# A diffusion layer on one core: split head sums, gated weight columns, a second store queue, and an order for pooled differences

## The chip, the core and the metric

The kernel runs on one core of a Trainium2 chip, as one launch. The metric is the time of one execution on the device in microseconds (us). A core has engines that run side by side and wait for one another through semaphores. In the profile PE is the matrix engine (TensorE), PEld its weight loads, DVE the vector engine, ACT the scalar engine, POOL the GpSimd engine and SP the engine that here issues nearly all DMAs. "SPq" marks what an engine's queue issues or waits for, a DMA for example.

## The reference

One trunk layer over 256 latent tokens and 256 context tokens of width 2048, all in float32. The parts that matter here, with the reference's own names:

```
h   = modulate(x, ...);  p = h @ w_in            # q, k, v, pool input, gate logits
heads = diff_attention(q, k_all, v_all, lam)     # 8 heads, value width 128
heads = rmsnorm(heads, subln_w) * (1 - lam_init) # mean of squares over the 128 values of a head
y_a = heads @ w_a_up
y_b = multiscale_pool(p[pool], ...) @ w_b_up     # 4 groups, windows 2, 4, 8, 16
x   = x + ga * ((g_a * y_a + g_b * y_b) @ w_o)
x   = x + gm * (square(relu(modulate(x, ...) @ w_ff1)) @ w_ff2)
```

`multiscale_pool` takes, for each token and each window, the mean of the input over the window (fewer tokens at both ends of the sequence) minus the input itself, and multiplies the difference by a 256 x 256 matrix of its group. `ga` and `gm` are vectors of 2048 gates that a product with `w_mod` makes.

## The kernel before

**Numbers in two halves.** PE multiplies operands of type fp32r faster than plain float32 ones. So most float32 operands are split: `hi` is the value cast to fp32r (ACT, line 245 for weights) and `lo` the rest (DVE, line 246). A product is three: hi·hi, lo·hi and hi·lo (`mm3`, lines 275 to 278, and `xstat`, lines 454, 455 and 460).

**Weights as a stream.** All weights come in chunks of 128 x 1024 floats (512 KB) in an order written out by hand (`plan`, lines 133 to 173). `load_next` (line 199) takes the next one: SP starts the DMA into one of 6 `raw` buffers, ACT casts it into one of 3 `whi` buffers, DVE subtracts into one of 3 `wlo` buffers. A chunk is loaded two chunks ahead of its use. Beside the stream a generator (`late_gen`, line 597) loads 128 chunks of `w_mod` for the gates; DVE accumulates them (`late_part`, lines 628 and 630), and POOL folds the rows with DMAs. `wchunk` calls `tick` once for each chunk, and work given to `later(n, ...)` comes up n chunks later.

**Stages.** First the modulation of both token sets with part of q and k (to about 190 us), then the other projections, attention and pooling side by side with the gates' products (to about 660 us), the output product `w_o`, and eight blocks of the MLP, each `ff1` (16 chunks) and then `ff2` (16 chunks: four groups `g` of 512 columns, four chunks each). Attention is a generator that `run` (line 871) advances between the matmuls of the other parts.

**Order.** A planner puts the instructions of each engine in order at build time: of those that it believes ready it takes the one that stands first in the program. Instructions passed through `pin` keep their program order among the pinned ones of the same engine. On the chip each engine then runs its list strictly in that order, and an instruction that waits holds up all behind it on its engine.

**The places that the change touches.**

- Head sums: `av` (line 715) makes two heads into one PSUM bank `ob`. ACT copies it (`osb`, 725) and squares it (`osq`, 727), POOL clamps the squares (728). Five chunks later `norm` multiplies them by `mean`, a 128 x 128 tile filled with 1/128, in one float32 product (732); ACT and DVE make a reciprocal root of it (`rsq`) and scale the heads.
- Pooled differences: `pooling` (764) makes a group's input in one bank, ACT copies it into two `za` tiles (787), POOL adds shifted copies of it (792). Four chunks later (eight for the last window) `pool_diff` (797) corrects the first tokens (803, pinned), the last ones (805, not pinned, windows 4 to 16) and subtracts the input (807, not pinned).
- Last block: POOL first multiplies the sums `acc` by `gm` and adds `x1` (1079, 1080). For each group of columns, `ff2` multiplies the bank by `gm` (1067), adds `acc` (1068) and stores (1069, SP's queue). The last group, g = 3, does so in two halves of 256 columns for each of the two token tiles, and its last two chunks are taken together (`last=2`), so that the first token tile is ready before the second.
- `work` tiles (line 75) are 9 buffers of 128 x 512 floats that attention, pooling and the head sums share.

Of the kernel before, what the change touches and what calls it, by code (L numbers as in the profile page):

```python
# [11 lines left out]
F32 = mybir.dt.float32  # L12
F32R = mybir.dt.float32r
AF = mybir.ActivationFunctionType
ALU = mybir.AluOpType
AX = mybir.AxisListType

P = 128
D = 2048
KT = D // P  # L20
T = 256
# [3 lines left out]
SQ_MAX = 3.39e38  # L25
# [23 lines left out]
def layer(ctx: ExitStack, tc, a, out):  # L49
    nc = tc.nc  # L50
    pool = ctx.enter_context(tc.tile_pool(name="sb", bufs=1))
    psum = ctx.enter_context(tc.tile_pool(name="ps", bufs=8, space=bass.MemoryType.PSUM))
    rows = ctx.enter_context(tc.tile_pool(name="rows", bufs=3, space=bass.MemoryType.DRAM))
    pe, gp = nc.tensor, nc.gpsimd
    pin = tc.keep_in_program_order
# [14 lines left out]
    act, vec, pe, sp = Engine(nc.scalar, ordered), Engine(nc.vector, ordered), Engine(nc.tensor, ordered_pe), nc.sync  # L70

    def bank(name):
        return psum.tile([P, 512], F32, tag="ps", name=name)

    def work(name, shape=None, dt=F32):
        return pool.tile(shape or [P, 512], dt, tag="w2", name=name, bufs=9)

    def s16(name, shape, dt=F32):
        return pool.tile(shape, dt, tag="s16", name=name, bufs=7)

    def s8(name, shape, dt=F32):
        return pool.tile(shape, dt, tag="s8", name=name, bufs=2)
# [7 lines left out]
    mods = {}  # L90
# [6 lines left out]
    def later(n, fn):  # L97

        waiting.append([n, fn])
# [15 lines left out]
    def raw_chunk(src, n=1024):  # L115
        raw = pool.tile([P, n], F32, tag="raw", name="raw", bufs=6)
        sp.dma_start(raw, src)
        return raw
# [61 lines left out]
    def x1_tile():  # L180
        if not x1s:
            x1s.append(s16("x1", [P, 2, D]))
        return x1s[0]
# [5 lines left out]
    def mod_raw(f, i):  # L189

        home = f % 2 if f > 7 else f % 4
        if home == 0:
            return pool.tile([P, 1024], F32, tag="raw", name="raw", bufs=6)
        n = 2 if home == 1 else 4
        if i % n == 0:
            wide[0] = (s8 if home == 1 else s16)("raw", [P, n, 1024])
        return wide[0][:, i % n, :]

    def load_next():
        key, rate = stream[len(loaded)]  # L200
        src = a[key[0]]
        for i in key[1:] if key[0] != "prq" else ():
            src = src[i]
        if key[0] == "prq":
            for dst, names in prq[key[1]]:
                nc.gpsimd.dma_start(dst, a["prq"][:, PRQ[names[0]][0]:PRQ[names[-1]][1]])
            loaded.append((key, None, None))
            return
        if key[0] in ("cT", "x"):
            dst = cT[:, 4 * key[1]:4 * key[1] + 4, :] if key[0] == "cT" else x1_tile()[:, key[1], key[2] * 512:key[2] * 512 + 512]  # L210
            nc.sync.dma_start(dst, src)
            loaded.append((key, None, None))
            return
        n = src.shape[-1]
        if key[0] == "w_m":
            raw = mod_raw(*key[1:])
            sp.dma_start(raw, src)
            loaded.append((key, raw, raw))
            return
        if key[0] in ("w_k", "w_q") and key[1] == 0:  # L220
            raw = pool.tile([P, n], F32, tag="aT", name="raw", bufs=2)
            sp.dma_start(raw, src)
            loaded.append((key, raw, raw))
            return
        raw = raw_chunk(src, n)
        if key == ("w_ff1a", 0):
            hi, lo = (pool.tile([P, n], F32R, tag="aT", name=nm, bufs=2) for nm in ("hi0", "lo0"))
        elif key == ("w_o", 3, 4):
            pair = s8("pair", [P, 2, 1024], F32R)
            hi, lo = pair[:, 0, :], pair[:, 1, :]  # L230
        elif key in (("w_ff1a", 2), ("w_ff1a", 3)):
            i = 2 * (key[1] - 2)
            if i == 0:
                early.append(s16("early", [P, 4, 1024], F32R))
            hi, lo = early[0][:, i, :], early[0][:, i + 1, :]
        elif key == ("w_ff1a", 1):
            halves = [[work(nm, dt=F32R) for nm in ("hi1", "lo1")] for _ in range(2)]
            for h in range(2):
                split(*halves[h], raw[:, h * 512:h * 512 + 512])
            loaded.append((key, *zip(*halves)))  # L240
            return
        else:
            hi = pool.tile([P, n], F32R, tag="whi", name="whi", bufs=3)
            lo = pool.tile([P, n], F32R, tag="wlo", name="wlo", bufs=3)
        act.copy(hi, raw)  # L245
        vec.tensor_sub(lo, raw, hi.bitcast(F32))  # L246
        loaded.append((key, hi, lo))
        credit[0] += rate if late[0] is not None else 0.0
        credit_rate[0] = rate
        while credit[0] >= 1.0:  # L250
            credit[0] -= 1.0
            if "gm" not in mods or mods["gm"] is not None or key[0] in ("w_ff1a", "w_ff1"):
                next(late[0], None)
# [17 lines left out]
    def split(hi, lo, src):  # L271
        act.copy(hi, src)  # L272
        vec.tensor_sub(lo, src, hi.bitcast(F32))  # L273
# [19 lines left out]
    prm = pool.tile([P, PRM_W], F32, tag="prm", name="prm")  # L293
# [12 lines left out]
    vec.memset(ebias, -32.0 * math.log(2.0))  # L306
    epsb = pool.tile([P, 1], F32, tag="epsb", name="epsb")
    vec.memset(epsb, EPS * 2.0 ** -64)
    mean = pool.tile([P, P], F32, tag="mean", name="mean")
    vec.memset(mean, 1.0 / P)  # L310


# [241 lines left out]
    for f in range(KT):  # L554
        if f % 2 == 0:
            ps = bank("mod")
# [158 lines left out]
    def av(h):  # L715
        assert h < values[0]
        if h % 2 == 0:
            ob[h // 2] = bank("ob")
        ps = ob[h // 2]
        for kc in range(4):  # L720
            pe.matmul(ps[:, (h % 2) * T:(h % 2) * T + T], v[:, kc, h * P:h * P + P], aTs[h][:, kc, :],
                      start=(kc == 0), stop=(kc == 3))
        if h % 2 == 1:
            osb = work("osb")
            act.copy(osb, ps)
            sq = work("osq")
            act.activation(sq, ps, AF.Square)
            gp.tensor_scalar(sq, sq, SQ_MAX, None, ALU.min)

            def norm():  # L730
                sp = bank("osum")
                pin(pe.matmul(sp, mean, sq, start=True, stop=True))
                r = rsq(sp, 512, 1.0)

                vec.scalar_tensor_tensor(r, sp, SUM_MAX / P, r, ALU.is_lt, ALU.mult)
                vec.scalar_tensor_tensor(osb, osb, sub8, r, ALU.mult, ALU.mult)
                o2 = osb.rearrange("p (a t) -> p a t", t=T)
                split(oT[:, 0, h - 1:h + 1, :], oT[:, 1, h - 1:h + 1, :], o2)
                heads[0] += 2

            later(5, norm)
# [55 lines left out]
    def pool_diff(g, w, ps, sums):  # L797

        d = work("d")
        n0, n1 = w // 2, w // 2 - 1  # L800
        e0 = PRM["edge"][0] + sum(x - 1 for x in WINDOWS[:g]) * 2
        for i, s in enumerate(sums):
            pin(vec.tensor_mul(s[:, 0:n0], s[:, 0:n0], prm[:, e0:e0 + n0]))
            if n1:
                vec.tensor_mul(s[:, T - n1:T], s[:, T - n1:T], prm[:, e0 + n0:e0 + n0 + n1])
            sl = slice(i * T, i * T + T)
            vec.scalar_tensor_tensor(d[:, sl], s, 1.0 / w, ps[:, sl], ALU.mult, ALU.subtract)
        diff.append((work("dh", dt=F32R), work("dl", dt=F32R)))
        later(1, partial(split, *diff[-1], d))

# [100 lines left out]
    for g in range(4):  # L911
        bs = [bank(f"wo{t}") for t in range(2)]
# [38 lines left out]
    acc = s16("acc", [P, 2, D])  # L951
# [98 lines left out]
    def ff2(b):  # L1050
        at = [acts[b]]
        for g in range(4):
            bs = [bank(f"f2_{t}") for t in range(2)]
            for _ in xstat(("w_ff2", b, g), bs, [(at, 0), (at, 1)], nk=4, last=2 if b == 7 and g == 3 else 1):
                pass
            gs = slice(g * 512, g * 512 + 512)
            for t in range(2):
                if b == 0:
                    act.copy(acc[:, t, gs], bs[t])
                elif b < 7:  # L1060
                    vec.tensor_add(acc[:, t, gs], bs[t], acc[:, t, gs])  # L1061
                else:
                    n = 256 if g == 3 else 512
                    for c in range(0, 512, n):
                        o = work("o", [P, n])
                        cs = slice(g * 512 + c, g * 512 + c + n)
                        vec.tensor_mul(o, bs[t][:, c:c + n], mods["gm"][:, cs])
                        vec.tensor_add(o, o, acc[:, t, cs])
                        nc.sync.dma_start(out[t * P:t * P + P, cs], o)

    ff1_first(bs)
    for b in range(8):
# [114 lines left out]
```

## Time and profile before

| | |
|---|---|
| median of 3 runs | 1454.63 us (1454.03 to 1455.06) |
| the profiled execution, its own time | 1452.88 us |
| its span, first to last instruction | 1451.0 us |
| PE busy | 1431.2 us (99%), 7448 matmuls |
| PEld busy | 1178.8 us (81%) |
| DVE busy | 975.3 us (67%) |
| ACT busy | 674.6 us (46%) |
| POOL busy | 173.4 us (12%) |
| DMA | 355.22 MB, mean 245 GB/s |

A row of a timeline has the start in us from the beginning of the span, the duration in us, the engine, the line, the operation, what it writes and reads, its shape and how many are merged in the row; in brackets stands for how long the engine was idle just before, and what ended that. A row of busy times by stretch has the stretch, its length, the busy us and the count of each engine, then the granted clock of PE, the busy share of the DMA engines and GB/s. Matmuls are pipelined, so a matmul's duration is longer than its distance from the next one. Both PE operand types are shown as f32 where they are inputs.

### The profile page before, as it was taken

To read this page: it belongs to the slowest core of one execution; us is meant where nothing else is said; L and a number is where in the kernel's file an instruction comes from. 1 tells how busy PE (TensorE), PEld (TensorE's weight loads), DVE (VectorE), ACT (ScalarE), POOL (GpSimd) and SP (SyncE) were. 2 spreads that over 40 slices of the span, in tenths; PEclk is the share of its full clock that TensorE was granted. 3 is DMA by queue.
4 is the path that set the end of the run, shared out by engine and by line. 5 is a ranking of instruction groups with operands and counts; after the bars stand their busy time and mean duration, and the time that the engine had idled before them with its cause. 6 is when DMAs were issued, how large, how long until landed. Compare 5 with 4: busy or idle time off the path is not lost.

```text
span 1451.0 us, 19755 instructions
## 1 busy us (share of the span) xinstructions
PE 1431.2 (99%) x7448; PEld 1178.8 (81%) x7448; DVE 975.3 (67%) x1218; ACT 674.6 (46%) x901; POOL 173.4 (12%) x192
## 2 busy tenths in 40 slices
PE   6999999999999999999999999999999999999998
PEld 4667887788888888888878888888888888888887
DVE  4567785668788778887766665656657555555675
ACT  5235345466644444444545545445354453544432
POOL 1001110101421111110101100011000110000260
PEclk9999999999999999999999999999999999999999
DMA  9996683345599999999746676777767765565563
GB/s 379 409 407 255 207 312 120 96 132 162 178 302 333 351 312 348 345 359 328 228 153 216 232 244 227 252 236 249 253 228 241 217 204 189 190 202 187 191 196 123
DMA packets 100975, 355.22 MB, mean 245 GB/s; under 512 B 12864, under 2 KB 13520, under 8 KB 100880
## 3 DMA queue, kind: packets, MB, share of 16 engines
q1 hardware_dynamic: 96624, 345.19, 68.8%
q0 software_dynamic: 4256, 8.77, 2.7%
q8 instruction: 58, 0.95, 0.3%
q14 instruction: 37, 0.30, 0.1%
HBM read 347.61 MB, written 2.17 MB: 241 GB/s over the span
## 4 chain that ended last, share of the span: by engine, by line
PE 91%; DMA 7%; DVE 1%; ACT 0%; issue 0%; SPq 0%; POOL 0%; DVEq 0%
PE f L1037 14%; PE f L455 8%; PE f L454 8%; PE f L460 8%; PE f L1039 7%; DMA raw<-in_w_m_dram 6%; PE pg L454 4%; PE pg L455 4%; PE pg L460 4%; PE pyy L454 2%; PE pyy L455 2%; PE pyy L460 2%; PE v L455 2%; PE v L454 2%; PE v L460 2%; PE wo L454 2%
## 5 line engine op out<-in xcount | busy, mean ns | idle before, releaser
L246 DVE TENSOR_TENSOR wlo<-raw,whi 128x1024 fp32r<-128x1024 f32 (+1 forms) x430 | 527.8, 1238 | 295.8 <-ACT whi L245 194.9
L245 ACT CAST whi<-raw 128x1024 fp32r<-128x1024 f32 (+1 forms) x430 | 450.4, 1048 | 519.3 <-PE f L455 183.8
L1037 PE MATMUL f<-h,whi 128*128 128x512 f32 x896 | 213.9, 391 | 0.0
L455 PE MATMUL f<-whi,act 128*128 128x512 f32 x512 | 199.3, 389 | 0.0
L454 PE MATMUL f<-whi,act 128*128 128x512 f32 x512 | 199.2, 389 | 0.0
L1037 PEld LDWEIGHTS f<-h,whi 128*128 128x128 f32 x896 | 165.0, 188 | 32.2
L460 PE MATMUL f<-wlo,act 128*128 128x512 f32 x512 | 136.8, 389 | 0.0
L1039 PEld LDWEIGHTS f<-h,wlo 128*128 128x128 f32 x896 | 114.9, 191 | 4.4
L1039 PE MATMUL f<-h,wlo 128*128 128x256 f32 x896 | 116.2, 283 | 0.0
L460 PEld LDWEIGHTS f<-wlo,act 128*128 128x128 f32 x512 | 96.1, 188 | 20.0
L455 PEld LDWEIGHTS f<-whi,act 128*128 128x128 f32 x512 | 96.2, 188 | 19.8
L454 PEld LDWEIGHTS f<-whi,act 128*128 128x128 f32 x512 | 96.1, 188 | 19.7
L454 PE MATMUL pg<-whi,hL 128*128 128x512 f32 x256 | 100.8, 394 | 0.0
L455 PE MATMUL pg<-whi,hL 128*128 128x512 f32 x256 | 99.7, 389 | 0.0
L1047 POOL TENSOR_TENSOR rsq<-relu 128x512 f32<-128x512 f32 x28 | 29.1, 1040 | 455.4 <-ACT relu L1046 445.2
L630 DVE SCALAR_TENSOR_TENSOR sb<-raw,sil,sb 128x1024 f32<-128x1024 f32 x60 | 76.7, 1278 | 0.0
L460 PE MATMUL pg<-wlo,hL 128*128 128x512 f32 x256 | 68.4, 389 | 0.0
L454 PEld LDWEIGHTS pg<-whi,hL 128*128 128x128 f32 x256 | 48.1, 188 | 10.5 <-ACT whi L245 0.4
L455 PEld LDWEIGHTS pg<-whi,hL 128*128 128x128 f32 x256 | 48.1, 188 | 10.1 <-issue 0.2
L460 PEld LDWEIGHTS pg<-wlo,hL 128*128 128x128 f32 x256 | 48.1, 188 | 10.0
L273 DVE TENSOR_TENSOR act<-rsq,act 128x512 fp32r<-128x512 f32 x28 | 19.3, 689 | 53.0 <-ACT act L272 53.0
L1061 DVE TENSOR_TENSOR acc<-f,acc 128x512 f32<-128x512 f32 x48 | 30.9, 686 | 20.4 <-PE f L460 20.4
(283 smaller groups left out, 2180.1 us busy)
## 6 DMA issues: line engine op xcount, KB each, us to landing
raw<-in_w_ff_dram SPq DMA_DIRECT2D x240, 512.0 KB, 4.3
raw<-in_w_m_dram SPq DMA_DIRECT2D x64, 512.0 KB, 10.2
raw<-in_w_ga_dram SPq DMA_DIRECT2D x32, 512.0 KB, 4.4
raw<-in_w_gb_in_dram SPq DMA_DIRECT2D x32, 512.0 KB, 5.3
raw<-in_w_cm_dram SPq DMA_DIRECT2D x32, 512.0 KB, 5.8
raw<-in_w_ga_in_dram SPq DMA_DIRECT2D x32, 512.0 KB, 5.6
raw<-in_w_sm_dram SPq DMA_DIRECT2D x32, 512.0 KB, 5.6
raw<-in_w_o_dram SPq DMA_DIRECT2D x32, 512.0 KB, 5.3
```

The lines of the kernel that those rows point to most:

```text
L245: act.copy(hi, raw)
L246: vec.tensor_sub(lo, raw, hi.bitcast(F32))
L273: vec.tensor_sub(lo, src, hi.bitcast(F32))
L454: pe.matmul(banks[t], tok(h, k, 0, tt), wt, start=k == 0, stop=False)
L455: pe.matmul(banks[t], tok(h, k, 1, tt), wt, start=False, stop=False)
L460: pe.matmul(banks[t], tok(h, k, 0, tt), wt, start=False, stop=k == 2 * nk - 1)
L630: pin(vec.scalar_tensor_tensor(o, raw, sil[:, 0, k:k + 1], o, ALU.mult, ALU.add))
L1037: pe.matmul(ps, hi[:, kk * P:kk * P + P], both(h2, k), start=k == 0, stop=False)
L1039: pe.matmul(ps[:, T:2 * T], los[k // 8][:, k % 8 * P:k % 8 * P + P], act_slice(h2, k, 0), start=False, stop=k == KT - 1)
L1047: gp.tensor_mul(sq, r, r)
L1061: vec.tensor_add(acc[:, t, gs], bs[t], acc[:, t, gs])
```

## The change

Four edits:

1. **Head sums.** POOL's clamp goes. DVE makes two fp32r tiles from the squares, `sh` (clamped) and `sl` (the rest of the clamped square), and `norm` multiplies both by the mean tile, now of type fp32r, into the same bank: two products for one float32 product.
2. **Gated weights.** When one of the last four chunks (`w_ff2`, block 7, g = 3) has landed, DVE multiplies it in place by the 512 gates `gm` of its columns, ahead of the cast. The last group's bank then needs only the addition of `acc`.
3. **Store.** The second half of each of the last group's two stores is issued on ACT's queue, the rest stays on SP's.
4. **Pooled differences.** Lines 805 and 807 are pinned like line 803.

```
+        if key[:3] == ("w_ff2", 7, 3):
+            r3 = raw.rearrange("p (k f) -> p k f", k=2)
+            vec.tensor_mul(r3, r3, mods["gm"][:, 1536:2048].unsqueeze(1).broadcast_to([P, 2, 512]))
...
-    mean = pool.tile([P, P], F32, tag="mean", name="mean")
+    mean_r = pool.tile([P, P], F32R, tag="mean", name="mean")
+    mean = mean_r.bitcast(F32)
...
-            gp.tensor_scalar(sq, sq, SQ_MAX, None, ALU.min)
+            sh, sl = (work(nm, dt=F32R) for nm in ("osh", "osl"))
+            vec.tensor_scalar(sh, sq, SQ_MAX, None, ALU.min)
+            vec.scalar_tensor_tensor(sl, sq, SQ_MAX, sh.bitcast(F32), ALU.min, ALU.subtract)
...
-                pin(pe.matmul(sp, mean, sq, start=True, stop=True))
+                pin(pe.matmul(sp, mean_r, sh, start=True, stop=False))
+                pin(pe.matmul(sp, mean_r, sl, start=False, stop=True))
...
-                vec.tensor_mul(s[:, T - n1:T], s[:, T - n1:T], prm[:, e0 + n0:e0 + n0 + n1])
+                pin(vec.tensor_mul(s[:, T - n1:T], s[:, T - n1:T], prm[:, e0 + n0:e0 + n0 + n1]))
...
-            vec.scalar_tensor_tensor(d[:, sl], s, 1.0 / w, ps[:, sl], ALU.mult, ALU.subtract)
+            pin(vec.scalar_tensor_tensor(d[:, sl], s, 1.0 / w, ps[:, sl], ALU.mult, ALU.subtract))
...
-                        vec.tensor_mul(o, bs[t][:, c:c + n], mods["gm"][:, cs])
-                        vec.tensor_add(o, o, acc[:, t, cs])
-                        nc.sync.dma_start(out[t * P:t * P + P, cs], o)
+                        if g < 3:
+                            vec.tensor_mul(o, bs[t][:, c:c + n], mods["gm"][:, cs])
+                            vec.tensor_add(o, o, acc[:, t, cs])
+                        else:
+                            vec.tensor_add(o, bs[t][:, c:c + n], acc[:, t, cs])
+                        (nc.scalar if c > 0 else nc.sync).dma_start(out[t * P:t * P + P, cs], o)
```

## The prediction

> **What bounds the kernel now.** I read the page's busy times and its chain of waits first, then the busy times by stretch, and then the timelines of the places that the change touches.
>
> ```profile
> PE 1431.2 (99%) x7448; PEld 1178.8 (81%) x7448; DVE 975.3 (67%) x1218; ACT 674.6 (46%) x901; POOL 173.4 (12%) x192
> ...
> PE 91%; DMA 7%; DVE 1%; ACT 0%; issue 0%; SPq 0%; POOL 0%; DVEq 0%
> ```
>
> ```profile
> 0.00:50.00 50.00, 37.62 (x285) 24.79 (x286) 25.00 (x56) 22.75 (x37) 5.89 (x15) 0.93 0.99 387
> ...
> 200.00:300.00 100.00, 99.46 (x453) 74.76 (x452) 66.74 (x121) 49.06 (x94) 8.21 (x5) 1.00 0.43 137
> 300.00:400.00 100.00, 99.27 (x641) 86.01 (x640) 76.96 (x115) 64.10 (x112) 24.84 (x41) 1.00 0.52 162
> 400.00:500.00 100.00, 100.00 (x452) 83.12 (x451) 79.57 (x77) 45.32 (x52) 17.55 (x22) 1.00 0.96 327
> ...
> 1400.00:1451.00 51.00, 46.34 (x205) 38.04 (x203) 31.19 (x37) 15.06 (x15) 8.14 (x5) 0.98 0.44 145
> ```
>
> PE carries the chain. It is idle for 12.4 us in the first 50 (50 minus 37.62), which the change doesn't touch, for some 1.3 us between 200 and 400 us, and for 4.7 us at the end. So only three things can make this kernel faster: less work on PE, the stalls between 200 and 400 us, and the tail. And anything that makes PE wait costs its full length. The span of 1451.0 us with 1.9 us around it is the profiled time, 1452.88; the median of the runs, 1454.63, is 1.75 above it. I make the sum against the profile and take the difference off the median.
>
> **Head sums, on PE.** The fourth of the four products, and its neighbours:
>
> ```profile
> 396.40 0.39 PE L455 MATMUL pg<-whi,hL 128*128 128x512 f32 x1
> 396.63 1.07 PE L460 MATMUL pg<-wlo,hL 128*128 128x512 f32 x4
> 397.54 1.02 PE L732 MATMUL osum<-osq,mean 128*128 128x512 f32 x2
> 397.99 0.79 PE L454 MATMUL pg<-whi,hL 128*128 128x512 f32 x1
> ```
>
> The product before ends at 397.70 (396.63 plus 1.07), the float32 product at 398.56 (397.54 plus 1.02): 0.86 us. An fp32r product of the same shape costs 0.23, the distance of the first two rows' starts. Two of them are 0.46, so 0.40 is saved each time, 1.6 us in four. Bounds: nothing, if fp32r against the mean tile ran no faster, to 2.5 us, if the second product hid wholly (4 times 0.63); all fp32r rows of this shape go at 0.23, so I take 1.6. The products stay pinned on PE, so they now wait for DVE where they waited for POOL.
>
> **Head sums, on DVE and POOL.** Nearest rows for the two new DVE steps are a one-source step of twice the width and a two-source step of the same width; what POOL loses stands below:
>
> ```profile
> L628 DVE TENSOR_SCALAR gm_bc<-raw,sil x2: 748/748/748, 766.5 to 955.8; 128x1024 f32<-128x1024 f32 x2
> L288 DVE SCALAR_TENSOR_TENSOR rq_t<-osum,rq_t x4: 684/690/691, 314.8 to 401.3; 128x512 f32<-128x512 f32 x4
> L728 POOL TENSOR_SCALAR osq<-osq x4: 1491/1559/2480, 282.6 to 388.6; 128x512 f32<-128x512 f32 x4
> ```
>
> `sh` is half of 748, some 0.4, and `sl` 0.69: 1.1 us for each pair of heads, 4.4 us on DVE, for 6 to 7 us less on POOL. The shortest time from squares to product is the third pair's:
>
> ```profile
> 363.46 1.57 POOL L728 TENSOR_SCALAR osq<-osq 128x512 f32<-128x512 f32 x1 [14.52 <-ACT osq L727]
> ...
> 368.23 1.02 PE L732 MATMUL osum<-osq,mean 128*128 128x512 f32 x2
> ```
>
> The squares exist by 363.4 and the product starts at 368.23. 1.1 us fits into 4.8, so I cost it at nothing. If the cover is gone, the pinned product waits and PE with it, at most 1.1 us a pair. The two tiles take one `work` buffer more through those five chunks; that is a risk below.
>
> **Pooled differences.** This is the one place in the attention stage where PE waits for long:
>
> ```profile
> DVE za L805 <- POOL za L792: 5.9, 3, 3.0
> ...
> PE pin L278 <- DVE wlo L246: 0.7, 1, 0.7
> ```
>
> ```profile
> 364.61 0.68 DVE L246 TENSOR_TENSOR wlo<-raw,whi 128x512 fp32r<-128x512 f32 x1
> 368.25 0.75 DVE L805 TENSOR_TENSOR za<-za,prm 128x3 f32<-128x3 f32 x2 [2.96 <-POOL za L792]
> 368.94 1.23 DVE L246 TENSOR_TENSOR wlo<-raw,whi 128x1024 fp32r<-128x1024 f32 x1
> ...
> 369.21 0.28 PE L277 MATMUL pin<-hL,whi 128*128 128x256 f32 x1
> 370.22 0.39 PE L278 MATMUL pin<-hL,wlo 128*128 128x256 f32 x1 [0.73 <-DVE wlo L246]
> 370.44 0.28 PE L276 MATMUL pin<-hL,whi 128*128 128x256 f32 x1
> ```
>
> The planner put line 805, which is not pinned, far ahead of its group's line 803. It holds DVE for 2.96 us until POOL's sums are done; the subtraction of the next weight chunk, behind it, comes at 368.94, though DVE was through with all else at 365.3 (364.61 plus 0.68), and PE stops. The two PE products ought to follow at 0.12 (369.33 and 369.45); the second comes at 370.44: 1.0 us lost. Pinned behind 803, line 805 comes where its sums have long been there. DVE gets back 5.9 us, which more than pays for the 4.4 above, and PE 1.0. Line 807 depended on 803 already, so its pin moves little; behind it wait `late_part` steps with their raw buffers, and each group's steps are 0.7 us longer in one piece (two small multiplications move there). What is late next is the same subtraction, 1.1 us later than it could be because the third pair's `sh` and `sl` come just ahead of it: at about 366.4 it is done by 367.6, 1.7 us before PE needs it at 369.33. Bounds: nothing, if another wait stands there, to 1.3 us, all the idle of that stage; I take 1.0.
>
> **Gated weights.** What counts is whether four multiplications of about 1.22 us (the price of line 246, same shape) find room ahead of their casts.
>
> ```profile
> 1429.15 1.05 ACT L245 CAST whi<-raw 128x1024 fp32r<-128x1024 f32 x1 [1.66 <-PE f L455]
> ...
> 1437.31 1.06 ACT L245 CAST whi<-raw 128x1024 fp32r<-128x1024 f32 x1 [1.66 <-PE f L455]
> ```
>
> ```profile
> 1430.24 1.22 DVE L246 TENSOR_TENSOR wlo<-raw,whi 128x1024 fp32r<-128x1024 f32 x1 [1.31 <-ACT whi L245]
> 1432.96 1.23 DVE L246 TENSOR_TENSOR wlo<-raw,whi 128x1024 fp32r<-128x1024 f32 x1 [1.50 <-ACT whi L245]
> 1435.04 1.29 DVE L1067 TENSOR_TENSOR o<-f,gm_bc 128x512 f32<-128x512 f32 x2 [0.86 <-PE f L460]
> ...
> L117 SPq DMA_DIRECT2D raw<-in_w_ff_dram x4: 327/334/340, 1416.9 to 1423.3; - x4
> ...
> DMA to landing us min/median/max: 3.4/3.7/3.8
> ```
>
> The last chunk is issued at 1423.3 and lands by 1427.1; its cast starts only at 1437.31, because a `whi` buffer is free no sooner. DVE idles 1.31, 1.50 and 0.86 us just there, so the multiplications go into gaps while the chunk lies waiting. PE needs the last chunk's `hi` half some 3.4 us after that cast ends (it begins the group four chunks of 2.72 us ahead of its end at 1446.34, that is at 1435.46, and takes the last chunk's first products two chunks and four products later, 6.35 us). So I cost them at nothing; uncovered, in a strict row of subtraction, multiplication and cast (3.5 us against 2.72 a chunk, four times), they would cost 3.2 less the 3.4 of slack, about nothing too, and one whole multiplication at the worst.
>
> **The tail.**
>
> ```profile
> 1445.27 1.07 PE L460 MATMUL f<-wlo,act 128*128 128x512 f32 x4
> 1446.38 0.76 DVE L1067 TENSOR_TENSOR o<-f,gm_bc 128x256 f32<-128x256 f32 x2 [1.30 <-PE f L460]
> 1447.05 0.75 DVE L1068 TENSOR_TENSOR o<-o,acc 128x256 f32<-128x256 f32 x2
> 1447.38 0.42 DVE L1068 TENSOR_TENSOR o<-o,acc 128x256 f32<-128x256 f32 x1
> 1447.91 0.38 SPq L1069 DMA_DIRECT2D out_dram<-o  x1
> ```
>
> From 1446.38 two multiplications and two additions run; without the multiplications the additions begin where 1067 did, 0.67 us sooner (1447.05 minus 1446.38). The second store is issued 0.11 after its addition ends (1447.80), so a queue of its own can win 0.1 here, and lose 0.3 to 0.4 if ACT issues half as fast as SP's 0.38. I take 0.7 for both edits; bounds 0.3 and 1.0.
> The Trainium skill (DMA: Bandwidth & Descriptors, section "Issuing engines are not separate DMA queues") says that a second issuing engine saves only the sequencer's time to start the DMA. By that rule alone the store edit would be worth at most one issue of 0.38, and no more from the transfer; the row leaves still less, 0.1.
>
> **Sum.** 1.6 plus 1.0 plus 0.7 is 3.3 us: span 1447.7, profiled time 1449.6, median of the runs 1451.3.
>
> **The rivals.**
>
> *The DMA stretch eats it (20%).* Between 410 and 690 us the transfers run at 0.97 of their engines, and once PE has no margin left:
>
> ```profile
> 410.00:550.00 140.00, 139.99 (x626) 115.79 (x625) 107.91 (x102) 58.07 (x63) 20.71 (x28) 1.00 0.97 332
> ...
> 548.75 0.19 PEld L454 LDWEIGHTS pg<-whi,hL 128*128 128x128 f32 x1 [0.43 <-ACT whi L245]
> ```
>
> If the transfers come no sooner, the 2.6 us won before 410 are waited for at 549, and only the tail stays: 1453.9. Against it: from 300 to 400 us the share is 0.52, so the stretch begins when buffers come free, which follows PE, and 0.97 leaves 4 us in 140.
>
> *A new block in DVE's order (12%), the other side.* The planner makes a new list from the first head sum on, and one `work` buffer fewer is free. An unpinned step that lands too early, as line 805 did, holds DVE for up to 3.0 us. Where PE has no margin (about 549 us) that costs PE all of it. One such block gives 1454.3, no change; two make the kernel slower, 3.3 minus 6.0, 1457.3. It decides from about 6.2 us of new stalls on. For it: DVE is busy 77% from 300 to 400 and 80% from 400 to 500. Against: DVE's own waits shrink by 5.9.
>
> *The pins don't do it (10%).* Another wait stands where line 805's stood: 1.0 less, 1452.3.
>
> *More comes free (8%).* The new order also clears the rest of the 1.3 us of idle between 200 and 400 us and the wait at 549: another 0.7, 1450.6.
>
> **How the numbers follow.** Forecast 50%, with a range of its own of 1450.3 to 1452.3 (the bounds of the tail and the stall). A change of 0.2%, 2.9 us, is about what a measurement of this kernel tells from none, that is 1451.7. The forecast lies just beyond it: I count 38 of its 50 as faster and 12 as the same. With 8 of the last rival, faster is 46; same is 12, 20 and 10, 42; slower is 12. The range reaches from 1449.5 (all three terms at their upper bounds, 2.5, 1.3 and 1.0, give 1449.8; the runs scatter by 0.5 around their median) to 1455.3 (the DMA rival or one block, with the lower bound of the tail and the same scatter); it leaves out the two blocks and little else.
>
> **What would show it.** Products at line 732's place 0.46 us apart from their neighbours instead of 0.86; no wait of DVE at line 805 and no idle PE near 370; the additions starting within 0.05 us of PE's last product, and the span ending some 4.0 us after it instead of 4.7; and, for the DMA rival, a longer wait of PEld for `whi` between 500 and 600 us. I would be wrong if PE shows new waits for DVE or `whi` of more than 1 us between 280 and 700 us, or if casts of the last four chunks wait for the multiplication beyond their slack.

## The result, and the profile after

The changed kernel takes 1450.64 us (median of 11 runs, 1449.45 to 1451.47); the kernel before took 1454.45 in the runs beside it (11 runs, 1452.53 to 1455.91). The ratio is 0.9978, with a 95% interval from 0.9970 to 0.9986: by the ratio 3.2 us faster, between 2.0 and 4.4 (the two medians alone lie 3.8 apart). The prediction was 1451.3, 3.3 us faster. The total came out. What did not are two of its smaller terms and the pricing of each edit by itself, and that is what the experiments are about.

The page of the changed kernel, its busy times:

```profile
span 1448.7 us, 19759 instructions
...
PE 1430.3 (99%) x7448; PEld 1179.3 (81%) x7448; DVE 984.1 (68%) x1226; ACT 674.4 (47%) x901; POOL 173.6 (12%) x188
```

The span is 2.3 us shorter. Where the time went is read best between fixed points of PE's work. These are starts (for the last, the end) of PE's products in the two timelines, counted from the first product of v, because the start of the kernel, which is paced by transfers, differs by itself: v began at 124.28 before and at 124.81 after, and at 125.61 in a second execution of the changed kernel. The tail goes by the span, which is given to 0.1 us.

| us from the first product of v to | before | after | difference |
|---|---|---|---|
| the first product of pg (377.81; 376.17) | 253.53 | 251.36 | -2.17 |
| the first product of wo (647.71; 646.02) | 523.43 | 521.21 | -2.22 |
| the end of the last product (1446.34; 1444.66) | 1322.06 | 1319.85 | -2.21 |
| tail: from there to the end of the span | 4.66 | 4.04 | -0.62 |

On balance all of PE's gain is made ahead of pg, and it is unchanged behind the next 270 us, most of which run with the transfers nearly saturated. On balance, because the fourth head sum's saving and two waits lie in that part too; they come below. The head sums, in the changed kernel's PE timeline:

```profile
395.63 1.07 PE L464 MATMUL pg<-wlo,hL 128*128 128x512 f32 x4
396.54 0.39 PE L738 MATMUL osum<-osh,mean 128*128 128x512 f32 x1
396.77 0.39 PE L739 MATMUL osum<-osl,mean 128*128 128x512 f32 x1
397.00 0.40 PE L458 MATMUL pg<-whi,hL 128*128 128x512 f32 x1
```

From 396.54 to 397.00 the pair of products takes 0.46. The pooled differences, in DVE's, POOL's and PE's timelines:

```profile
365.18 0.68 DVE L249 TENSOR_TENSOR wlo<-raw,whi 128x512 fp32r<-128x512 f32 x1
366.65 4.54 DVE L249 TENSOR_TENSOR wlo<-raw,whi 128x1024 fp32r<-128x1024 f32 x3 [0.79 <-ACT whi L248]
...
365.52 7.19 POOL L799 TENSOR_TENSOR za<-za 128x271 f32<-128x271 f32 x6
...
368.56 0.28 PE L280 MATMUL pin<-hL,whi 128*128 128x256 f32 x1
368.68 0.28 PE L281 MATMUL pin<-hL,wlo 128*128 128x256 f32 x1
```

DVE goes straight on to the subtractions while POOL is still adding, and PE's `pin` products follow at 0.12. The first of the three subtractions lasts 1.39 and ends at 368.04, 0.64 ahead of the product that needs it (368.68). PE waits elsewhere instead, in the view of PE's waits and its timeline with DVE's beside it:

```profile
PE pd L280 <- DVE dl L276: 0.4, 1, 0.4
...
381.85 0.28 PE L279 MATMUL pd<-dh,whi 128*128 128x256 f32 x1
382.51 0.39 PE L280 MATMUL pd<-dl,whi 128*128 128x256 f32 x1 [0.38 <-DVE dl L276]
382.73 0.28 PE L281 MATMUL pd<-dh,wlo 128*128 128x256 f32 x1
382.85 0.28 PE L279 MATMUL pd<-dh,whi 128*128 128x256 f32 x1
...
380.63 1.22 DVE L249 TENSOR_TENSOR wlo<-raw,whi 128x1024 fp32r<-128x1024 f32 x1
381.77 0.69 DVE L276 TENSOR_TENSOR dl<-d,dh 128x512 fp32r<-128x512 f32 x1
```

Three products that ought to take 0.36 take 1.00 (381.85 to 382.85): 0.64 lost, because `dl` of the third window ends at 382.46. The tail and the gated weights:

```profile
1443.59 1.07 PE L464 MATMUL f<-wlo,act 128*128 128x512 f32 x4
1444.77 0.76 DVE L1078 TENSOR_TENSOR o<-f,acc 128x256 f32<-128x256 f32 x2 [1.96 <-PE f L464]
1445.56 0.34 ACTq L1079 DMA_DIRECT2D out_dram<-o  x1
...
1419.44 2.44 DVE L228 TENSOR_TENSOR raw<-raw,gm_bc 128x1024 f32<-128x1024 f32 x2 [0.53 <-DMA raw<-in_w_ff_dram]
1427.60 2.35 DVE L228 TENSOR_TENSOR raw<-raw,gm_bc 128x1024 f32<-128x1024 f32 x2
...
1435.63 1.06 ACT L248 CAST whi<-raw 128x1024 fp32r<-128x1024 f32 x1 [1.62 <-PE f L459]
```

The four multiplications stand in two pairs, the last ending at 1429.95, and the last chunk's cast still waits for PE's `whi` buffer, not for them. The last additions begin 0.11 after PE's last product (1444.77 after 1444.66).

### The profile page after: what moved, and what is told of

It is laid out like the page before. It is cut to its first block, busy times and chain, and to the rows that moved or that the text cites. A ratio compares the mean times of both kernels' runs of the same rounds, so it can differ in the third digit from the quotient of the medians.

```text
span 1448.7 us, 19759 instructions
## 1 busy us (share of the span) xinstructions
PE 1430.3 (99%) x7448; PEld 1179.3 (81%) x7448; DVE 984.1 (68%) x1226; ACT 674.4 (47%) x901; POOL 173.6 (12%) x188
## 3 DMA queue, kind: packets, MB, share of 16 engines
HBM read 347.61 MB, written 2.17 MB: 241 GB/s over the span
## 4 chain that ended last, share of the span: by engine, by line
PE 95%; DMA 4%; DVE 0%; ACT 0%; issue 0%; SPq 0%; DVEq 0%
PE f L1044 14%; PE f L459 8%; PE f L458 8%; PE f L464 8%; PE f L1046 7%; PE pg L458 4%; PE pg L459 4%; PE pg L464 4%; DMA raw<-in_w_m_dram 2%; PE w_k L68 2%; PE pyy L458 2%; PE pyy L459 2%; PE pyy L464 2%; PE v L459 2%; PE v L458 2%; PE v L464 2%
```

## The experiments

The kernels ran four to a chip, each beside the kernel before. The fixed points of all profiles, as in the table above:

| kernel | ratio to before, 95% interval | v to pg | pg to wo | v to last product | tail |
|---|---|---|---|---|---|
| before | | 253.53 | 269.90 | 1322.06 | 4.66 |
| changed | 0.9978, 0.9970 to 0.9986 | 251.36 | 269.85 | 1319.85 | 4.04 |
| changed, once more | 0.9981, 0.9972 to 0.9990 | 251.36 | 269.86 | 1319.66 | 4.03 |
| pins undone | 1.0003, 0.9994 to 1.0012 | 254.31 | 269.20 | 1321.90 | 4.04 |
| head sums undone | 0.9986, 0.9977 to 0.9995 | 252.54 | 271.28 | 1322.22 | 4.08 |
| gates and store undone | 0.9983, 0.9974 to 0.9992 | 251.37 | 269.97 | 1320.35 | 4.62 |
| store undone | 0.9980, 0.9971 to 0.9989 | 251.37 | 270.21 | 1320.00 | 4.04 |
| before, pins alone | 1.0000, 0.9991 to 1.0009 | 252.54 | 269.79 | 1320.75 | 4.66 |
| before, head sums alone | 1.0005, 0.9996 to 1.0014 | 254.37 | 270.16 | 1324.11 | 4.64 |
| products of v left out | 0.9899, 0.9885 to 0.9913 | 238.45 | 270.71 | 1308.78 | 4.02 |
| 8 work buffers | 0.9985, 0.9976 to 0.9995 | 251.37 | 271.49 | 1321.79 | 4.06 |
| pd one chunk later | 0.9994, 0.9985 to 1.0002 | 251.36 | 272.12 | 1321.86 | 4.42 |
| pd behind ob | 0.9983, 0.9974 to 0.9992 | 251.37 | 270.31 | 1320.15 | 4.37 |
| third window's differences sooner | 0.9971, 0.9960 to 0.9983 | 251.36 | 269.34 | 1319.47 | 4.08 |

The first column of times repeats within 0.01 wherever the order of instructions up to there is the same (within 0.06 for pins undone and head sums alone), so it can be trusted to a tenth; the second can't, as shown below.

**Pins undone**

```diff
-                pin(vec.tensor_mul(s[:, T - n1:T], s[:, T - n1:T], prm[:, e0 + n0:e0 + n0 + n1]))
+                vec.tensor_mul(s[:, T - n1:T], s[:, T - n1:T], prm[:, e0 + n0:e0 + n0 + n1])
...
-            pin(vec.scalar_tensor_tensor(d[:, sl], s, 1.0 / w, ps[:, sl], ALU.mult, ALU.subtract))
+            vec.scalar_tensor_tensor(d[:, sl], s, 1.0 / w, ps[:, sl], ALU.mult, ALU.subtract)
```

> The changed kernel with lines 805 and 807 unpinned again (the pins undone, all else kept). I measure PE's stretch, from the start of the first product of v to the end of PE's last product: 1322.06 us before (124.28 to 1446.34), 1319.85 in the changed kernel (124.81 to 1444.66). My theory: DVE waits for POOL's sums at the unpinned step near 365 us again, and PE stops near 370 for about 1.0; in exchange the changed kernel's new wait of PE for dl at 382 us (0.64 lost) goes, since PE comes there 1 us later. So the stretch is some 0.4 longer than with the pins, 1320.2, and the DVE waits at that step sum to 4 to 6 us. Rival, the pins buy the full 1.0: 1320.9. Rival, the pins buy nothing because the next wait takes all of it: 1319.9.

The runs show no gain any more: ratio 1.0003, and pg comes 2.95 us later than in the changed kernel. That is more than even the rival with the full 1.0. The wait at 382 us is gone, as I expected, and with it pg to wo is 0.65 shorter. Its timelines, of POOL, DVE and PE:

```profile
364.73 0.10 POOL L792 MEMSET za<- 128x8 f32 x1 [16.52 <-DVE osl L734]
365.48 3.79 POOL L799 TENSOR_TENSOR za<-za 128x271 f32<-128x271 f32 x6
...
368.72 0.74 DVE L812 TENSOR_TENSOR za<-za,prm 128x3 f32<-128x3 f32 x2 [2.90 <-POOL za L799]
369.41 3.50 DVE L249 TENSOR_TENSOR wlo<-raw,whi 128x1024 fp32r<-128x1024 f32 x3
...
370.69 0.39 PE L281 MATMUL pin<-hL,wlo 128*128 128x256 f32 x1 [2.45 <-DVE wlo L249]
```

DVE is held for 2.90, about as before, but PE stands for 2.45 instead of 0.73. PE goes on when the subtraction behind the held step is done, and that moment hangs on POOL's sums, not on PE. Whatever PE has won by then, it waits away.

**Head sums alone**, the other side of the same, with the theory that the run above suggested. The edit, in the kernel before:

```diff
...
-            gp.tensor_scalar(sq, sq, SQ_MAX, None, ALU.min)
+            sh, sl = (work(nm, dt=F32R) for nm in ("osh", "osl"))
+            vec.tensor_scalar(sh, sq, SQ_MAX, None, ALU.min)
+            vec.scalar_tensor_tensor(sl, sq, SQ_MAX, sh.bitcast(F32), ALU.min, ALU.subtract)
...
-                pin(pe.matmul(sp, mean, sq, start=True, stop=True))
+                pin(pe.matmul(sp, mean_r, sh, start=True, stop=False))
+                pin(pe.matmul(sp, mean_r, sl, start=False, stop=True))
```

> The kernel before with only the head sums changed. My theory now: PE's stop near 370 us ends when DVE is released by POOL's sums, at a moment that PE's own head start doesn't move. So the three savings ahead of it (1.2 us) lengthen that stop from 1.0 to about 2.5, and the first product of pg comes no sooner after the first product of v than before (253.53 us): 253.5 to 254.5. What is left is the fourth saving, 0.4, at the most: the kernel is not faster. Rival, as the prediction summed it: each edit keeps its own worth, 252.3, and the kernel is 1.6 us faster.

```profile
PE pin L278 <- DVE wlo L246: 2.5, 1, 2.5
...
370.46 0.75 DVE L809 TENSOR_TENSOR za<-za,prm 128x3 f32<-128x3 f32 x2 [2.90 <-POOL za L796]
371.16 3.50 DVE L246 TENSOR_TENSOR wlo<-raw,whi 128x1024 fp32r<-128x1024 f32 x3
...
367.22 3.80 POOL L796 TENSOR_TENSOR za<-za 128x271 f32<-128x271 f32 x6
```

POOL's sums in the kernel before:

```profile
365.20 3.60 POOL L792 TENSOR_TENSOR za<-za 128x271 f32<-128x271 f32 x6
```

It is not faster (1.0005), and pg comes 0.84 us later than before. The subtractions begin at 371.16, that is 245.51 after the first product of v (125.65); in the kernel before they began at 368.94, 244.66 after it. They are 0.85 later, and so is pg: PE's restart is DVE's, to 0.01. With the pins undone it is the same: subtractions 245.45 after the first product of v, pg 8.86 behind them as here. The 0.85 comes from POOL's sums: counted from the first product of v they start 0.65 later (241.57 against 240.92) and take 0.20 longer. The reason for the later start lies in shared buffers, by the releasers that the profile names: the row of POOL above (pins undone) shows the first `za` buffer waiting for `sl` on DVE, and the second waits for `dl` behind it, where in the kernel before both followed POOL's own clamp. So the clamp's move to DVE does have a price at this place, and the pins take it off the path too.

**Pins alone**

```diff
-                vec.tensor_mul(s[:, T - n1:T], s[:, T - n1:T], prm[:, e0 + n0:e0 + n0 + n1])
+                pin(vec.tensor_mul(s[:, T - n1:T], s[:, T - n1:T], prm[:, e0 + n0:e0 + n0 + n1]))
...
-            vec.scalar_tensor_tensor(d[:, sl], s, 1.0 / w, ps[:, sl], ALU.mult, ALU.subtract)
+            pin(vec.scalar_tensor_tensor(d[:, sl], s, 1.0 / w, ps[:, sl], ALU.mult, ALU.subtract))
```

> The kernel before with only the two pins of the pooled differences. My theory: DVE's waits for POOL's sums at line 805 (5.9 us) and PE's stop near 370 (1.0) go; dl at 382 is on time within 0.1, since PE comes there only 1.0 earlier: PE's stretch from the first product of v to the last product is 1.0 shorter than before's 1322.06, so 1321.1, and the tail stays at 4.66. Rival, another wait takes the place of that one: 1321.6 to 1322.1.

pg is 0.99 sooner, as the stop of 1.0 says. The stretch is 1.31 shorter in the profile; the runs don't show it (1.0000, the interval reaches down to 0.9991, which is 1.3 us). So at pg the head sums alone are worth -0.84, the pins alone 0.99, and both together 2.17.

**Head sums undone**

```diff
...
-            sh, sl = (work(nm, dt=F32R) for nm in ("osh", "osl"))
-            vec.tensor_scalar(sh, sq, SQ_MAX, None, ALU.min)
-            vec.scalar_tensor_tensor(sl, sq, SQ_MAX, sh.bitcast(F32), ALU.min, ALU.subtract)
+            gp.tensor_scalar(sq, sq, SQ_MAX, None, ALU.min)
...
-                pin(pe.matmul(sp, mean_r, sh, start=True, stop=False))
-                pin(pe.matmul(sp, mean_r, sl, start=False, stop=True))
+                pin(pe.matmul(sp, mean, sq, start=True, stop=True))
```

> The changed kernel with the head sums as before (POOL clamps, one float32 product each). My theory: each product costs 0.86 instead of 0.46 again; three of them lie ahead of the new wait of PE at 382 us, which shrinks to nothing when PE comes 1.2 later, so the stretch from the first product of v to the last product is 1.6 less 0.64, about 1.0 longer, 1320.8. Rival, the four savings add up in full whatever stands behind them: 1321.5. Rival, the head sums' saving is hidden (the transfers from 410 to 690 us pace PE): 1319.9. In all cases the tail after PE's last product stays at 4.04.

pg is 1.18 later: three times 0.40, as expected. The whole stretch is 2.37 longer, not 1.0, and the rest lies between pg and wo, mostly in PEld's waits for the casts of chunks that land late (for the first, the chunk landed at 445.21 and its cast began at 445.31):

```profile
446.41 0.19 PEld L457 LDWEIGHTS pyy<-whi,oT 128*128 128x128 f32 x1 [0.71 <-ACT whi L248]
477.73 0.19 PEld L457 LDWEIGHTS pyy<-whi,yb 128*128 128x128 f32 x1 [0.57 <-ACT whi L248]
494.64 0.19 PEld L457 LDWEIGHTS pg<-whi,hL 128*128 128x128 f32 x1 [0.70 <-ACT whi L248]
```

The kernel with the pins alone has the same order of instructions on every engine until the last group of columns, and it went through this part in 269.79 where this one took 271.28. So up to 1.5 us of this part is not the program's; it differs between executions (these two ran on different chips). The same holds for pins undone and head sums alone: their orders agree until the last group, and they took 269.20 and 270.16 here and differ by another 1.2 behind wo, where PE waits 0.86 for `whi` in the second. A profile's total can't settle terms below that, and a part that repeats to 0.01, like the one ahead of pg, can. The runs, 0.9986, don't separate this kernel from the changed one.

**Gates and store undone**

```diff
-        if key[:3] == ("w_ff2", 7, 3):
-            r3 = raw.rearrange("p (k f) -> p k f", k=2)
-            vec.tensor_mul(r3, r3, mods["gm"][:, 1536:2048].unsqueeze(1).broadcast_to([P, 2, 512]))
...
-                        if g < 3:
-                            vec.tensor_mul(o, bs[t][:, c:c + n], mods["gm"][:, cs])
-                            vec.tensor_add(o, o, acc[:, t, cs])
-                        else:
-                            vec.tensor_add(o, bs[t][:, c:c + n], acc[:, t, cs])
-                        (nc.scalar if c > 0 else nc.sync).dma_start(out[t * P:t * P + P, cs], o)
+                        vec.tensor_mul(o, bs[t][:, c:c + n], mods["gm"][:, cs])
+                        vec.tensor_add(o, o, acc[:, t, cs])
+                        nc.sync.dma_start(out[t * P:t * P + P, cs], o)
```

(All four groups are multiplied by `gm` behind PE's products again.)

> The changed kernel with the gated weights and the store on ACT's queue undone, so that the last columns are multiplied after PE's last product as before. My theory: PE's stretch stays at 1319.85 within 0.1, and from PE's last product to the end of the span it is 4.66 again instead of 4.04. Rival, the multiplications of the weights cost PE something that is given back here: a stretch more than 0.2 shorter.

The tail is 4.62 again, as expected. PE's stretch is 0.5 longer than in the changed kernel, 0.12 of it between pg and wo and the rest behind wo, where PE waits 0.30 for `whi` at 727 us. Neither my theory nor the rival has that sign. The orders of all engines are those of the changed kernel until the last group of columns, so the wait at 727 is a difference between executions and not a price. The runs, 0.9983, can't separate it from 0.9978.

**Store undone**

```diff
-                        (nc.scalar if c > 0 else nc.sync).dma_start(out[t * P:t * P + P, cs], o)
+                        nc.sync.dma_start(out[t * P:t * P + P, cs], o)
```

> The changed kernel with both stores of the last columns on SP's queue, gated weights kept. My theory: the second queue saves what the last store waits behind the first, 0.1: from PE's last product to the end of the span 4.1 to 4.2 instead of 4.04. Rival, a queue of its own saves a whole issue: 4.4. Rival, issuing on ACT's queue costs as much as it saves: 4.0 or less.

The tail is 4.04, as with ACT's queue. Its last rows:

```profile
1444.26 0.76 DVE L1078 TENSOR_TENSOR o<-f,acc 128x256 f32<-128x256 f32 x2 [1.96 <-PE f L464]
...
1445.14 0.39 SPq L1079 DMA_DIRECT2D out_dram<-o  x1
```

The last store is issued 0.12 after the addition ends (1445.02), against 0.03 with ACT's queue (1445.56 after 1445.53). The 0.1 that the prediction gave the second queue is there at the issue and not at the end of the span: from issue to landing the last store took 2.2 with ACT's queue and 2.1 on SP's. The second queue is worth nothing measurable.

**A head start of 13 us.** The rival that the transfers eat the gain, tested with more than the change can give; the products of the inputs' lo halves are left out of the second half of v:

```diff
-                            pe.matmul(banks[t], tok(h, k, 1, tt), wt, start=False, stop=False)
+                            if w != ("w_v", 1):
+                                pe.matmul(banks[t], tok(h, k, 1, tt), wt, start=False, stop=False)
```

> The changed kernel, and the products of the inputs' lo halves in the second half of v are left out: 64 products of 0.23 us between about 247 and 304 us, 14.5 us less work of PE. It asks whether a head start won ahead of the stretch in which the transfers are 0.97 busy (410 to 690 us) comes through it. I compare the start of the first product of pg (376.17 in the changed kernel), of the first product of wo (646.02) and the end of the last product (1444.66), each counted from the first product of v. My theory: whatever head start shows at pg, 10 to 14.5 us, shows at wo and at the end within 1 us. Rival, the transfers pace that stretch by themselves: less than half of it is left at wo, and PEld waits for whi between 500 and 650 us for the rest.

The head start is 12.91 at pg, 12.05 at wo (521.21 less 509.16) and 11.07 at the last product. PE's and PEld's waits name the two losses:

```profile
PE wo L68 <- ACT whi L248: 0.9, 1, 0.9
PE pyy L458 <- ACT whi L248: 0.5, 1, 0.5
...
PEld pyy L458 <- ACT whi L248: 1.0, 1, 1.0
```

86% of a head start six times that of the change arrives; at the end it missed my bound of 1 us by 0.8. The stretch is not paced by the transfers alone, it moves with PE, and the transfers take a nibble out of what passes.

**8 work buffers**

```diff
-        return pool.tile(shape or [P, 512], dt, tag="w2", name=name, bufs=9)
+        return pool.tile(shape or [P, 512], dt, tag="w2", name=name, bufs=8)
```

> The changed kernel with 8 instead of 9 of the shared work buffers. It prices the one buffer more that the new sums hold. My theory: the buffers are not what PE waits for; PE's stretch stays within 0.5 of 1319.85. Rival, they are short: one fewer costs PE new waits of 1 us or more between 200 and 420 us, so that the new sums' extra buffer is a price of the change.

Nothing changes ahead of pg (251.37). Behind it the stretch is 1.94 longer, so my bound of 0.5 was missed, with one wait of PEld for `whi` of 1.28 at 493 us, where executions differ anyway. The new waits of the rival, between 200 and 420 us, are not there. DVE, ACT and POOL got other orders with the edit, so it doesn't test the buffer alone, and the runs (0.9985 against 0.9981 for the changed kernel on another chip) don't separate the two. Neither side is shown, beyond that a buffer less doesn't cost PE anything in attention up to pg.

**Getting back the 0.64 at 382 us, three ways.** First, pd one weight chunk later:

```diff
-                    if g == 0 and gname == "w_gb_in" and ch == 1:
+                    if g == 0 and gname == "w_gb_in" and ch == 2:
                         pool_out(2)
```

(The load of `pool_w` is moved along in the stream.)

> The changed kernel with the third group's product of the pooled differences (pd, at 382 us) one weight chunk later, 2.7 us of other products ahead of it. My theory of where a part of the expected gain stayed: PE came to this product 1.64 us sooner than before, but dl was only 0.95 sooner, so 0.64 was waited for. Then here the wait is gone and PE's stretch is 1319.2, 0.6 shorter than in the changed kernel. Rival, DVE is the bound there and the wait moves on to the next weight chunk's lo half: 1319.9.

Second, pd behind the attention step:

```diff
+                    yield w
                     if g == 0 and gname == "w_gb_in" and ch == 1:
                         pool_out(2)
-                    yield w
```

> The changed kernel with the third group's product of the pooled differences (pd, at 382 us) issued behind the attention step that follows it instead of ahead of it: 0.9 us or more of PE's work (ob) comes ahead of pd, and no chunk of the stream moves. My theory: the 0.64 us that PE waits there for dl is gone, and where no wait for whi is added, the stretch from the first product of v to the last product is 0.6 shorter, 1319.2. Rival: as with pd one chunk later, the new order of DVE and ACT costs more behind it than it wins: 1319.9 or longer.

Both remove the wait at 382 and both get another one, of the same kind, at the fourth group's product:

```profile
PE pd L279 <- ACT dh L275: 0.8, 1, 0.8
```

The planner made other lists for ACT and DVE behind the moved product, in which the fourth group's `dh` is late: 0.64 won, 0.8 lost. My theory missed both times. The second is 0.3 longer than the changed kernel, as its rival said; the first 2.0, with four waits of PEld for `whi` of 2.3 together besides. The tail, too, went from 4.04 to about 4.4: the last additions begin 0.46 after PE's last product in both, and why is open. Third, the differences of the third window a chunk sooner, so that `dl` comes sooner:

```diff
-            later(4 if g < 3 else 8, partial(pool_diff, g, w, ps, sums))
+            later((4, 4, 3, 8)[g], partial(pool_diff, g, w, ps, sums))
```

> The changed kernel with the pooled differences of the third window three chunks after its sums instead of four. It puts a pinned step where POOL's sums have not ended yet (about 369 us). My theory: DVE is held for 1 to 3 us there as by the unpinned step before the change, the subtraction of a weight chunk behind it is late, and PE loses 0.5 to 2 us near 372, though dl at 382 is then early. The pin itself is not what helps; that DVE doesn't meet POOL's sums early is. Rival: a pinned step is harmless wherever it stands: the stretch is 0.6 shorter, as dl comes sooner.

My theory fell. DVE is held by POOL's sums as I said, but PE doesn't notice:

```profile
367.32 2.96 DVE L249 TENSOR_TENSOR wlo<-raw,whi 128x1024 fp32r<-128x1024 f32 x2 [0.79 <-ACT whi L248]
371.39 0.57 DVE L810 TENSOR_TENSOR za<-za,prm 128x4 f32<-128x4 f32 x1 [1.12 <-POOL za L799]
...
378.13 1.12 DVE L276 TENSOR_TENSOR dl<-d,dh 128x512 fp32r<-128x512 f32 x1
```

Two weight subtractions stand ahead of the held step here, not behind it; the hold is 1.12, and `dl` ends at 379.2 instead of 382.5, so pd doesn't wait. This is the fastest of the kernels that leave nothing out: 1449.28 us (6 runs), ratio 0.9971 with an interval from 0.9960 to 0.9983, against 1451.10 and 0.9981 for the changed kernel beside it on the same chip. The intervals overlap, so that it is faster than the changed kernel is not shown. In the profile pg to wo is 0.51 shorter, as with the pins undone, where the wait at 382 was gone too; of that 0.2 to 0.4 are left in the whole stretch against the two profiles of the changed kernel.

**The changed kernel once more**

> The changed kernel once more, beside the others on the same chip. My theory: its profile repeats 251.36 us from the first product of v to the first product of pg within 0.1, since the transfers don't pace that part, and the stretch from the first product of pg to the first product of wo (269.85) differs by up to 1.5 us from one execution to the next, since PE's margin over the transfers is thin there. Rival: that stretch repeats within 0.3, and what the other kernels showed there is theirs.

pg repeats to 0.01, as expected, and so, against my expectation, does the part from pg to wo (269.86 and 269.85). For these two executions the rival is right: PE met no wait for the transfers there. Store undone and gates undone, with the same orders up to wo, took 270.21 and 269.98. So this order spread by 0.4 in four executions, where the order without the new head sums spread by 1.5 in two; that it arrives with more margin over the transfers would explain it and is not shown.

## Why the prediction was right, and where it was not

- **What bounds the kernel.** Right: PE's gain is the kernel's gain, and the runs (3.2 us) agree with the two profiles' 2.21 on PE plus 0.62 in the tail, 2.83, within their interval. That interval, 2.0 to 4.4, can't tell 2.8 from the 3.3 of the sum; by the profiles the PE part is 0.4 short of its 2.6, for the reason given below under what is late next.
- **Head sums on PE, 0.40 each.** Right: 0.46 for a pair of products; undoing them moves pg by 1.18 for three.
- **Head sums on DVE, costed at nothing.** Right only with the pins. The two steps cost what was said (0.42 and 0.69), and no product of the head sums waited for them. But without the pins POOL's sums start later behind `sl`, and pg comes 0.84 later than before, in spite of three savings on PE.
- **Pooled differences, 1.0.** The size is right for the pins alone (0.99), and with both edits in the kernel the sum is right at pg: three times 0.40 and 1.0 make 2.2, and 2.17 was measured. The step that failed is the independence: the prediction treated 1.6 and 1.0 as if each were kept whatever became of the other. Without the pins the head sums bring nothing at pg, and with the head sums in the kernel the pins are worth 2.95. The rival "the pins don't do it" was priced by this mistake, at 1.0 less; undoing them cost 2.95 at pg and, in the runs, all of the gain.
- **What is late next.** The prediction named the subtraction at 366 us, and said that 1.7 us of margin were left; 0.64 were, since PE came there 1.2 sooner by the three head sums ahead of it, which that margin had left out. It was enough. It did not see `dl` at 382 us, which before the change had been just in time (382.28 and 1.13 long against the product that needed it at 383.61). Counted from the first product of v, PE now comes 2.17 sooner and `dl` ends only 1.48 sooner, so PE waits: 0.64 lost. That is about the size of what the part behind pg won, the fourth head sum's 0.40 and the wait at 549 us, which vanished.

```profile
382.28 1.13 DVE L273 TENSOR_TENSOR dl<-d,dh 128x512 fp32r<-128x512 f32 x1
...
383.61 0.28 PE L277 MATMUL pd<-dl,whi 128*128 128x256 f32 x1
```

- **Gated weights, at nothing.** Right: no cast waited for a multiplication.
- **The tail, 0.7.** 0.62. It comes from the multiplications alone: their 0.67, less the 0.07 by which the additions begin later after PE's last product than the multiplications did (0.11 against 0.04; the prediction asked for 0.05). The 0.1 of the second queue did not show.
- **The DMA rival.** That the transfers eat the whole gain is refuted by the 13 us that came through to 86%; what is true in it are waits of PE for `whi` of 0.2 to 0.9 us in single executions.
- **A new block in DVE's order.** It did not come. What the fourth edit takes away is the old block, which the new head sums make longer: in the kernel with edits 1 to 3 DVE waits 6.7 us for POOL at line 812, against 5.9 before, in three waits.

```profile
DVE za L812 <- POOL za L799: 6.7, 3, 2.9
```

- **The range.** Its bounds are not those that it names: 1.6, with 0 to 1.3 for the stall and 0.3 to 1.0 for the tail, gives 1450.7 to 1452.7, not 1450.3 to 1452.3. The measured 1450.64 is inside the range as stated and just outside this one.

## What to carry to other kernels

Before adding up savings on the bounding engine, look at each place where it waits and ask what ends that wait: where it is another engine's chain, all that is saved ahead of it goes into the wait, and an edit that frees the chain is worth the wait plus everything saved ahead of it. So price such edits together, and look for operands that were just in time before, for they are the next wait. Undo each edit from the finished kernel and also make it alone; the two answers differ exactly where edits depend on one another.

## What the runs showed of the hardware

POOL's six additions (128x265 to 128x271) took 3.79 us while DVE was held (pins undone) and 7.19 while DVE subtracted beside it (changed kernel), and three subtractions on DVE took 4.54 instead of 3.50. I had not expected the freed DVE to slow POOL to half. The two additions of 128x269, in pins undone and in the changed kernel, with the mean ns of one behind the busy time:

```profile
L799 POOL TENSOR_TENSOR za<-za 128x269 f32<-128x269 f32 x2 | 1.2, 632 | 0.0
...
L799 POOL TENSOR_TENSOR za<-za 128x269 f32<-128x269 f32 x2 | 3.2, 1613 | 0.0
```

With the third window's differences sooner, both durations stand in one execution: 1.61 us each beside DVE's subtractions and 0.63 each while DVE was held. The Trainium skill (SBUF — State Buffer, section "Who interferes with whom") says that a DVE instruction with two SBUF inputs contends with a GpSimd instruction that reads SBUF; both kinds stand here side by side, and the trace agrees, with 0.35 us more for each of DVE's subtractions and 0.98 for each of these additions of POOL.
